# Weight loads, sums and splits lifted above elementwise work in a recurrent layer, and one three-quarter sum loaded earlier

## The chip, the cores and the metric

The kernel runs on one core of a Trainium2 chip. The metric is the device time of one execution in microseconds (us); less is better. The core has five engines with a queue each: TensorE (PE, matrix products), VectorE (DVE) and ScalarE (ACT) for elementwise work, GpSimd (POOL), and SyncE (SP), which here only starts DMA transfers. GpSimd starts transfers too, in this kernel those that add to what lies in the destination.

## The reference

One inference step of a two-layer trunk, for a prompt of 512 frames and 8 decoding sequences of 16 frames, cut here to the recurrent layer that the change touches; the second layer is a stick-breaking attention over a shared key and value cache.

```python
D_MODEL, D_RNN, N_GATE_BLOCKS, CONV_W = 2048, 4096, 16, 4

def recurrent_mixer(hn, h0, conv0, w_in, conv_w, conv_b, w_r, b_r, w_i, b_i, lam, w_out):
    xb, zg = jnp.split(hn @ w_in, 2, axis=-1)          # 2048 -> 2 x 4096
    xb, conv_new = causal_conv(xb, conv0, conv_w, conv_b)
    y, hT = rg_lru(xb, h0, w_r, b_r, w_i, b_i, lam)
    return (y * jax.nn.silu(zg)) @ w_out, hT, conv_new

def rg_lru(x, h0, ...):
    r = jax.nn.sigmoid(block_diag(x, w_r, b_r)); i = jax.nn.sigmoid(block_diag(x, w_i, b_i))
    log_a = -8.0 * r * jax.nn.softplus(-lam)
    a, u = jnp.exp(log_a), jnp.sqrt(-jnp.expm1(2.0 * log_a)) * (i * x)
    # h_t = a_t * h_(t-1) + u_t along the frames
    ...

# per layer: hn = rms_norm(x, g_pre) * (1 + scale) + shift, with (shift, scale, gate) = silu(c) @ w_ada + b_ada  (adaLN)
#            x = x + gate * rms_norm(mixer(hn), g_post)
```

All data are fp32.

## The kernel before

Every fp32 product is made of three matmuls on a split into a high and a low part: high by high (L101), high by low (L102), low by high (L103). `hilo` makes the split of a weight tile: ScalarE writes `wh` (L87), VectorE writes `wl` (L88). Four pairs of `wh`/`wl` are in rotation (`WB = 4`), so splits run at most four tiles ahead of TensorE. `ahead()` draws them from a plan; `weights()` hands out the next one.

The kernel is written in a framework that orders the instructions of each engine at compile time: an instruction goes out by its priority, which follows the order of the code, once its inputs can be there; `high_priority(n)` moves what is written inside it n places up, and `issue_after` holds one instruction behind another. Tiles of one tag share a fixed number of buffers, so a load into a tile waits for the last reader of the tile before.

The stages: a prologue (0 to about 131 us) in which `start` normalises x, reads the adaLN weights (`wa`) and, per block k of 16, projects the first output blocks with `w_first` (`wf`) as they come; the recurrent stage (about 131 to 1080 us); then the output projection and the attention layer, which the change leaves alone.

The recurrent stage works on pairs of feature blocks (256 features), j = 0 to 15: the z-half (`silu_gates`), the recurrence (`lru`) and the x-half (`inputs`) of the next pair with its `conv`. Each half is one `pair_product`: a Winograd scheme for a 2 by 2 block product in seven products instead of eight, on sums of the quarters of the weights. Its order on TensorE is X11, S1, S2, X12, a plain part, S3, X22, a plain part, S4, plain parts. The banks `pa7` and `pc7` are used again, so ScalarE first copies them out (`keep`, L546); VectorE then adds the copies to the other banks (`evac`, to `hb` in the x-half, L616, or to `zs` in the z-half, L661).

The weight sums lie in tiles by tag: `r11` and `r2` one quarter, `t1` and `t3` two, `t2` (x-half) and `u2` (z-half) three, and a fourth later. The first quarter is a plain load on SP's queue (`big_load`, L471), every other one an adding transfer that GpSimd starts (`add`, L476). Two sums into one tile must follow each other. Each tile is loaded again as soon as its split is done. `rv` is the smaller weights.

In `lru`, per block: gates (L689), exponential (L699), tanh (L703) and root (L711) on ScalarE, the scan on VectorE (L723), then

```python
            G.tensor_copy(st[:, h, 0:1], r[:, TP - 1 : TP])                                  # L724
            G.tensor_copy(st[:, h, 1:9], r[:, TP:]...[:, :, TS - 1])                         # L725
            V.tensor_tensor(r, r, zs[h], ALU.mult)                                           # L726
            G.dma_start(self.yd[P * f : P * f + P, :], r)                                    # L727
        G.dma_start(self.O["state"][:, 2 * j : 2 * j + 2, :], st)                            # L728
```

GpSimd copies the final states out of the scan's result (in the trace `st<-g`), and VectorE multiplies that result in place by the gate branch, which has to wait for the copies. The products go to a scratch `yd` in memory. In the trace, tiles appear with their name's first part: `t` is `t1`, `t2` or `t3`, `u` is `u2`, `r` is `r11` or `r2`.

In the prologue, `wf` tiles take the buffers of the first five weight tags (`r11`, `t1`, `t2`, `r2`, `t3`) in turn.

## Time and profile before

| | us |
|---|---|
| three runs | 2930.27, 2933.09, 2934.37 |
| median | 2933.09 |
| the profiled execution | 2927.55 |
| its span | 2925.8 |

The span is what the profile covers from first to last instruction. In the rows of the profile, an engine's row gives busy time, share and count; a stretch gives its length and then the busy time of each engine, the granted TensorE clock (1.00 is full) and the DMA share; a single instruction gives start and duration, and in brackets the idle time before it and what ended that.

### The profile page before, as it was taken

The page shows a single profiled execution, that of the slowest core. Times are in us where ns is not written, and L with a number is a line of the kernel's source. Part 1 is how long each engine was busy: PE and PEld are TensorE (multiplying, and loading weights), DVE is VectorE, ACT ScalarE, POOL GpSimd, SP SyncE. Part 2 cuts the span into 40 slices and gives each one's busy share as a digit, 9 for nine tenths or more (in the row PEclk, how much of TensorE's full clock was granted, in tenths as well). Part 3 has the DMA queues.
Part 4 walks back from the last instruction along what each step waited for, and adds up shares of the span by engine and source line. Part 5 has one row for each costly group of instructions (what it writes and reads, how often), then busy time and mean ns, then how long its engine had stood idle before and what let it go on. Part 6 is the DMA issues. An engine that isn't in the chain of part 4 may idle for free.

```text
span 2925.8 us, 48667 instructions
## 1 busy us (share of the span) xinstructions
PE 2844.2 (97%) x18874; PEld 2532.5 (87%) x18874; DVE 1951.6 (67%) x2795; ACT 1601.4 (55%) x2459; POOL 445.9 (15%) x683
## 2 busy tenths in 40 slices
PE   7889999999999999999999999999999999999998
PEld 5789999999999987778778999878989999897887
DVE  7666776677667766724468877787666766667435
ACT  5456655665556556623456666674455555556323
POOL 0022232222222200001112322001100000001000
PEclk9989999999999999999999999999999999999999
DMA  9967788777777756555567666653665556656736
GB/s 333 328 161 179 178 193 198 173 174 196 192 188 172 180 162 209 175 138 172 175 223 259 215 213 214 206 198 108 198 186 176 182 170 188 193 170 188 218 105 226
DMA packets 263287, 564.07 MB, mean 193 GB/s; under 512 B 24440, under 2 KB 108536, under 8 KB 261904
## 3 DMA queue, kind: packets, MB, share of 16 engines
q1 hardware_dynamic: 232016, 465.60, 50.0%
q0 software_dynamic: 31040, 95.36, 15.6%
q8 instruction: 148, 2.42, 0.3%
q14 instruction: 83, 0.68, 0.1%
HBM read 523.76 MB, written 37.11 MB: 192 GB/s over the span
## 4 chain that ended last, share of the span: by engine, by line
PE 80%; DMA 9%; issue 4%; DVE 4%; POOL 2%; ACT 1%; SPq 0%; DVEq 0%; POOLq 0%; ACTq 0%
PE acc L101 7%; PE acc L102 7%; PE acc L103 7%; PE psh L101 5%; PE acck L101 5%; PE psh L103 5%; PE psh L102 5%; PE acck L103 5%; PE acck L102 5%; DMA u<-w_in_a_dram 4%; PE pa L101 2%; PE pa L103 2%; PE pa L102 2%; DMA t<-w_in_a_dram 2%; PE psa L198 2%
## 5 line engine op out<-in xcount | busy, mean ns | idle before, releaser
L88 DVE TENSOR_TENSOR wl<-wr,wh 128x1024 fp32r<-128x1024 f32 x216 | 269.7, 1249 | 290.6 <-ACT wh L87 287.7
L87 ACT ACTIVATE wh<-wr 128x1024 fp32r<-128x1024 f32 x216 | 228.2, 1056 | 382.4 <-PE acc L103 227.3
L101 PE MATMUL acc<-wh,yh 128*128 128x512 f32 x960 | 378.6, 395 | 8.0 <-ACT yh L764 4.7
L102 PE MATMUL acc<-wl,yh 128*128 128x512 f32 x960 | 377.2, 393 | 6.0 <-DVE wl L88 6.0
L103 PE MATMUL acc<-wh,yl 128*128 128x512 f32 x960 | 375.0, 392 | 1.2 <-DVE yl L765 1.2
L186 DVE TENSOR_TENSOR wa<-wa,wa 128x1024 bf16<-128x1024 f32 (+1 forms) x256 | 310.0, 1246 | 23.6 <-ACT wa L185 21.3
L101 PE MATMUL psh<-nh,wh 128*128 128x320 f32 x1024 | 323.9, 316 | 0.0
L103 PE MATMUL psh<-nh,wl 128*128 128x320 f32 x1024 | 318.9, 311 | 0.0
L102 PE MATMUL psh<-nl,wh 128*128 128x320 f32 x1024 | 317.5, 310 | 0.0
L185 ACT ACTIVATE wa<-wa 128x1024 bf16<-128x1024 f32 x256 | 263.5, 1052 | 60.7 <-DVE wa L186 46.7
L101 PEld LDWEIGHTS acc<-wh,yh 128*128 128x128 f32 x960 | 182.0, 190 | 55.9 <-issue 8.7
L102 PEld LDWEIGHTS acc<-wl,yh 128*128 128x128 f32 x960 | 182.0, 190 | 45.9 <-DVE wl L88 8.7
L103 PEld LDWEIGHTS acc<-wh,yl 128*128 128x128 f32 x960 | 181.4, 189 | 39.9 <-DVE yl L765 2.5
L101 PEld LDWEIGHTS psh<-nh,wh 128*128 128x128 f32 x1024 | 192.3, 188 | 19.3 <-DVE ql L1099 12.6
L101 PE MATMUL pa<-xs,wh 128*128 128x320 f32 x540 | 172.9, 320 | 20.8 <-ACT keep L546 17.5
L103 PEld LDWEIGHTS psh<-nh,wl 128*128 128x128 f32 x1024 | 192.4, 188 | 0.5 <-DVE wl L88 0.2
L102 PEld LDWEIGHTS psh<-nl,wh 128*128 128x128 f32 x1024 | 192.3, 188 | 0.1
L103 PE MATMUL pa<-xs,wl 128*128 128x320 f32 x540 | 169.4, 314 | 5.6 <-DVE wl L88 5.6
L102 PE MATMUL pa<-xs,wh 128*128 128x320 f32 x540 | 169.0, 313 | 0.0
L101 PE MATMUL acck<-nh,wh 128*128 128x320 f32 x512 | 161.5, 315 | 0.0
L476 POOL DMA_DIRECT2D t<-w_in_a_dram x105 | 93.1, 907 | 428.9 <-DMA t<-w_in_a_dram 247.1
L103 PE MATMUL acck<-nh,wl 128*128 128x320 f32 x512 | 158.3, 309 | 0.0
(353 smaller groups left out, 7420.3 us busy)
## 6 DMA issues: line engine op xcount, KB each, us to landing
wa<-w_ada_dram SPq DMA_DIRECT2D x192, 512.0 KB, 4.6
wr<-w_out_a_dram SPq DMA_DIRECT2D x96, 512.0 KB, 4.3
t<-w_in_a_dram POOLq DMA_DIRECT2D x105, 384.0 KB, 7.4
r<-w_in_a_dram SPq DMA_DIRECT2D x90, 384.0 KB, 5.9
wr<-w_in_b_dram SPq DMA_DIRECT2D x64, 512.0 KB, 5.2
ck<-cache_k_dram SPq DMA_DIRECT2D x64, 512.0 KB, 6.5
cv<-cache_v_dram SPq DMA_DIRECT2D x64, 512.0 KB, 5.3
t<-w_in_a_dram SPq DMA_DIRECT2D x75, 384.0 KB, 4.2
```

Of the source, the lines that this page charges most:

```text
L87: nc.scalar.activation(hi[:, :n], raw, AF.Copy)
L88: nc.vector.tensor_tensor(lo[:, :n], raw, hi[:, :n].bitcast(F32), ALU.subtract)
L101: mm(out, sh, mh, start=start, stop=False, **kw)
L102: mm(out, sh, ml, start=False, stop=False, **kw)
L103: mm(out, sl, mh, start=False, stop=stop, **kw)
L185: nc.scalar.activation(parts[i], raw, AF.Copy)
L186: nc.vector.tensor_tensor(parts[2] if i else raw, raw, parts[i], ALU.subtract)
L198: nc.tensor.matmul(ps[32 * j : 32 * j + 32, :], self.c3[:, 4 * g + j, :], ws[j // 2][i][:, j % 2, :], start=g + i == 0, stop=g == 3 and i ...
L476: self.nc.gpsimd.dma_start(t, self.quarter(w, i), accum_op=ALU.add)
```

## The change

Two edits. First, in the prologue, the `wf` tiles no longer use the buffer of `t2`, so that `t2` of the first pair can be loaded, and its two further quarters added, when block 8 of the adaLN weights is reached. The dictionary `big` of loaded tiles is made in `start` for that, and `plan` leaves out a tag that is loaded already. Second, in the recurrent stage, everything that `ahead()` draws from the plan, that is the splits, the loads into the tiles that they free, and the adding transfers, is put into `high_priority(200)`; after that stage the number is 0.

```diff
-        tags = list(self.BIG)[:5]
+        tags = [t for t in self.BIG if t not in ("t2", "u2")]
+        self.big = {}
...
+            if k == 8:
+                self.big_load("t2", self.I["w_in_a"][1])
...
-        self.big = {}
         at = [w[q] for q in order] + [None, None]
         for tag in self.BIG:
-            self.big_load(tag, at[tag == "u2"])
+            if tag not in self.big:
+                self.big_load(tag, at[tag == "u2"])
...
     def ahead(self, held=0):
 
-        for x in islice(self.planned, max(0, self.WB - held - len(self.ready))):
-            self.ready.append(x)
+        with self.tc.high_priority(self.urgent):
+            for x in islice(self.planned, max(0, self.WB - held - len(self.ready))):
+                self.ready.append(x)
...
-            self.WB, self.WW = 4, WQ
+            self.WB, self.WW, self.urgent = 4, WQ, 200
...
-            self.WB, self.RB, self.WW = 3, 4, 1024
+            self.WB, self.RB, self.WW, self.urgent = 3, 4, 1024, 0
```

The changed file's lines stand 2 to 5 further down: L471 becomes L475, L476 L480, L546 L551, L616 L621, L711 L716, L717 L722, L724 to L727 become L729 to L732. The instructions of all engines are the same in both kernels; their order differs. Three places in the recurrence of a middle pair, with the x-half of the next pair on TensorE. The first is GpSimd's queue, where `g_6237` and `g_6272` are the scan results of the pair's two blocks, `t3_6415` and `t2_6442` the weight sums to come. Before:

```order
L476 DMA t1_6227<-w_in_a_dram 128x768 [waits DMASW5_49,DMAHW5_49,DMASW1_49,DVE_49]
L476 DMA t2_5782<-w_in_a_dram 128x768 [waits DMASW3_49,DMASW2_49,DVE_49]
L724 COPY st_5954<-g_6237 128x1 [waits DVE_49]
L725 COPY st_5954<-g_6237 128x8
L727 DMA yd_65<-g_6237 128x640 [waits DVE_49]
L476 DMA t3_6415<-w_in_a_dram 128x768 [waits DMAHW0_49,DMASW6_49,Activation_49]
L724 COPY st_5954<-g_6272 128x1 [waits DVE_49]
L725 COPY st_5954<-g_6272 128x8
L476 DMA t2_6442<-w_in_a_dram 128x768 [waits DMAHW2_49,DMASW2_49,Activation_49]
```

After, at the same place of GpSimd's queue:

```order
L480 DMA t1_6227<-w_in_a_dram 128x768 [waits DMASW4_49,DMAHW5_49,DMASW1_49,DVE_49]
L480 DMA t2_5782<-w_in_a_dram 128x768 [waits DMASW2_49,DVE_49]
L480 DMA t3_6415<-w_in_a_dram 128x768 [waits DMASW6_49,DMAHW0_49,DMASW3_49,DVE_49]
L480 DMA t2_6442<-w_in_a_dram 128x768 [waits DMAHW1_49,DMASW2_49,DVE_49]
L729 COPY st_5954<-g_6237 128x1 [waits DVE_49]
L730 COPY st_5954<-g_6237 128x8
L732 DMA yd_65<-g_6237 128x640 [waits DVE_49]
L480 DMA t2_6442<-w_in_a_dram 128x768 [waits DMASW4_49]
L729 COPY st_5954<-g_6272 128x1 [waits DVE_49]
L730 COPY st_5954<-g_6272 128x8
```

The sums of the coming `t3` and `t2` moved up past the state copies, and the second sum of `t2`, which waits for the first to land (DMASW4), now stands ahead of the copies of the second block. The second place is VectorE's queue from the second block's scan on. Before:

```order
L723 SCALAR_TENSOR_TENSOR g_6272<-q_6320,g_6272 128x640 [waits DVE_49]
L616 TENSOR_TENSOR hb_6359<-pb7_6448,keep_6391 128x320 [waits PE_49]
L88 TENSOR_TENSOR wl_6506<-rv_6133,wh_6505 128x512 [waits DMAHW2_49,PE_49,Activation_49]
L726 TENSOR_TENSOR g_6272<-g_6272,zs_5982 128x640 [waits DVE_49,Pool_49]
L88 TENSOR_TENSOR wl_6512<-r11_6196,wh_6511 128x768 [waits DMAHW4_49,PE_49,Activation_49]
```

After, on VectorE's queue:

```order
L728 SCALAR_TENSOR_TENSOR g_6272<-q_6320,g_6272 128x640 [waits DVE_49]
L88 TENSOR_TENSOR wl_6506<-rv_6133,wh_6505 128x512 [waits DMAHW2_49,PE_49,Activation_49]
L731 TENSOR_TENSOR g_6272<-g_6272,zs_5982 128x640 [waits DVE_49,Pool_49]
L88 TENSOR_TENSOR wl_6512<-r11_6196,wh_6511 128x768 [waits DMAHW4_49,PE_49,Activation_49]
L621 TENSOR_TENSOR hb_6359<-pd7_6486,keep_6517 128x192 [waits PE_49]
L88 TENSOR_TENSOR wl_6538<-t1_6227,wh_6537 128x768 [waits DMASW1_49,Activation_49]
```

The in-place product of the second block (L726, now L731) keeps its place after the scan and its wait for GpSimd; the splits behind it moved up towards it. The third place is ScalarE's queue in the roots of the same pair, where `keep_6391` and `keep_6418` are the first two copies of the x-half, and `t3_6033` and `t2_5782` the weights of its S1 and S2. Before:

```order
L711 ACTIVATE g_6237<-g_6237 128x640 [waits DVE_49]
L711 ACTIVATE g_6272<-g_6272 128x640 [waits DVE_49,Activation_49]
L546 ACTIVATE keep_6391<-pa7_6365 128x320 [waits PE_49]
L87 ACTIVATE wh_6411<-t3_6033 128x768 [waits DMASW6_49,PE_49]
L717 ACTIVATE q_6318<-q_6318,mone_101 128x640 [waits DVE_49]
L717 ACTIVATE q_6320<-q_6320,mone_101 128x640 [waits DVE_49]
L546 ACTIVATE keep_6418<-pc7_6366 128x320 [waits PE_49]
L87 ACTIVATE wh_6438<-t2_5782 128x768 [waits DMASW2_49,PE_49]
```

After, on ScalarE's queue:

```order
L87 ACTIVATE wh_6411<-t3_6033 128x768 [waits DMASW6_49,PE_49]
L716 ACT_TABLE_LOAD
L716 ACTIVATE g_6237<-g_6237 128x640 [waits DVE_49]
L87 ACTIVATE wh_6438<-t2_5782 128x768 [waits DMASW2_49,PE_49]
L716 ACTIVATE g_6272<-g_6272 128x640 [waits DVE_49,Activation_49]
L551 ACTIVATE keep_6391<-pa7_6365 128x320
L722 ACTIVATE q_6318<-q_6318,mone_101 128x640 [waits DVE_49]
L551 ACTIVATE keep_6418<-pc7_6366 128x320
```

Both splits moved up, that of `t3` ahead of the roots and that of `t2` between them and ahead of the first `keep`.

## The prediction

> **What bounds the kernel now.** I read the page's head and its first table, then the stretches of the span by engine, then the waits and single rows of the recurrent stage, since the diff touches only the prologue and that stage. The page first.

> ```profile
> span 2925.8 us, 48667 instructions
> PE 2844.2 (97%) x18874; PEld 2532.5 (87%) x18874; DVE 1951.6 (67%) x2795; ACT 1601.4 (55%) x2459; POOL 445.9 (15%) x683
> ```

> TensorE is busy for 97% of the span, so a change in order can gain only what TensorE waits, and lose by new waits. Where it waits, by stretch (start:end, length, then busy time of each engine, granted clock, DMA share, GB/s):

> ```profile
> 131.00:160.00 29.00, 19.14 (x103) 18.48 (x102) 15.45 (x45) 11.60 (x23) 8.92 (x18) 0.82 0.94 214
> 185.00:240.00 55.00, 48.68 (x308) 47.44 (x307) 43.46 (x67) 39.31 (x58) 9.74 (x17) 0.91 0.56 137
> 540.00:600.00 60.00, 59.13 (x401) 58.63 (x401) 42.69 (x67) 35.26 (x54) 16.22 (x27) 1.00 0.76 185
> 600.00:660.00 60.00, 57.99 (x394) 57.50 (x393) 41.53 (x63) 35.20 (x53) 13.29 (x22) 1.00 0.74 178
> ```

> Two places lose: the first product (131 to 160), and the first whole pair (185 to 240). The steady stage loses 1 to 2 us in each 60. The waits of TensorE between 131 and 1075 us (total, times, longest):

> ```profile
> PE pa L101 <- ACT keep L546: 17.5, 14, 6.5
> PE pa L103 <- DVE wl L88: 5.6, 1, 5.6
> PE pa L101 <- ACT hb L611: 3.4, 1, 3.4
> ```

> The 14 waits on the copy `keep` are one of 6.50 us in the prologue and 13 of one kind, one in each later pair: 17.5 - 6.5 = 11.0 us, or 0.85 each. What a wait costs beside its own length shows in rows of single gaps (the bracket holds the idle time) and in the stretches of halved clock behind them:

> ```profile
> 140.63 0.41 PE L101 MATMUL pa<-xs,wh 128*128 128x320 f32 x1 [3.36 <-ACT hb L611]
> 154.20 0.64 PE L101 MATMUL pa<-xs,wh 128*128 128x320 f32 x1 [6.50 <-ACT keep L546]
> 204.31 0.63 PE L103 MATMUL pa<-xs,wl 128*128 128x320 f32 x1 [5.57 <-DVE wl L88]
> 621.24 0.42 PE L101 MATMUL pa<-xs,wh 128*128 128x320 f32 x1 [2.01 <-ACT keep L546]
> 1066.75 0.71 PE L101 MATMUL acc<-wh,yh 128*128 128x512 f32 x1 [2.49 <-ACT yh L764]
> ```

> ```profile
> 141.85:145.27 3.42, 3.42 (x15) 3.42 (x14) 0.93 (x6) 0.16 (x1) 0.82 (x5) 0.50 1.05 276
> 152.09:158.92 6.83, 4.72 (x18) 4.72 (x19) 5.73 (x8) 3.94 (x9) 2.66 (x6) 0.50 0.93 193
> 199.88:210.12 10.24, 5.81 (x22) 5.81 (x23) 10.00 (x17) 2.98 (x5) 4.15 (x10) 0.50 0.52 148
> 1066.87:1070.28 3.41, 3.41 (x9) 2.63 (x10) 3.41 (x9) 3.41 (x5) 0.00 (x0) 0.50 0.21 77
> 619.30:640.00 20.70, 18.76 (x128) 18.76 (x129) 10.17 (x14) 11.08 (x18) 2.59 (x3) 1.00 0.80 205
> ```

> After gaps of 2.49 us and more the granted clock is 0.50 for 3.4 us or a multiple of it; after the gap of 2.01 us it stays 1.00. At full clock matmuls of this shape start 0.147 us apart (18.76 us / 128), so 3.42 us hold 23; the first row has 15. A gap of some 2.5 to 4.5 us therefore costs about 8 x 0.147 = 1.2 us more.

> **The change, part by part.** The instructions are the same in number and kind; only the order changes, and only up to the end of the recurrent stage at some 1075 us. So every term is a wait won or lost.

> *Steady pairs, 13 of them (j = 1 to 13).* I take the pair whose x-half (`inputs`) starts on TensorE at E = 580.99, and count from there. GpSimd's queue carries both the adding transfers of the weights and the copies of the recurrence's state:

> ```profile
> 582.13 1.76 POOL L476 DMA_DIRECT2D t<-w_in_a_dram  x2 [7.41 <-DMA t<-w_in_a_dram]
> 595.24 0.91 POOL L724 COPY st<-g 128x1 f32<-128x1 f32 x1 [11.35 <-DVE h0t L720]
> 599.56 0.19 POOL L724 COPY st<-g 128x1 f32<-128x1 f32 x1 [0.62 <-DVE g L723]
> 602.39 0.87 POOL L476 DMA_DIRECT2D t<-w_in_a_dram  x1 [2.52 <-ACT wh L87]
> 610.18 0.90 POOL L476 DMA_DIRECT2D t<-w_in_a_dram  x1 [5.42 <-DMA t<-w_in_a_dram]
> 610.76 1.25 POOL L476 DMA_DIRECT2D u<-w_in_a_dram  x1
> ```

> ```profile
> 580.99 0.31 PE L101 MATMUL pa<-xs,wh 128*128 128x320 f32 x1
> 600.39 0.82 DVE L726 TENSOR_TENSOR g<-g,zs 128x640 f32<-128x640 f32 x1
> 610.48 0.42 ACT L546 ACTIVATE keep<-pa 128x320 f32<-128x320 f32 x1
> 612.03 0.31 PE L101 MATMUL pa<-xs,wh 128*128 128x320 f32 x1
> ```

> Before, both pairs of state copies (595.24 and 599.56) are through before the first sum of the next `t2` goes out (602.39). Its second sum goes out at 610.18, when the first has landed; since the same tile is summed twice, this wait is real. Behind it stand only the `u2` sum and others: that is the cause of the 2.01 us gap at 621.24, as the chain of waits shows, where the `u2` sum lands at 619.92 and its split and the `keep` follow:

> ```profile
> 602.39 7.23 DMA t<-w_in_a_dram
> 610.76 9.16 DMA u<-w_in_a_dram
> 620.77 0.43 ACT keep L546
> ```

> After, as the order of GpSimd shows, both sums of `t2` are pulled ahead of the second block's state copies. The second sum waits for the landing of the first with the copies behind it, and VectorE's second `g *= zs` (L726, then L731) waits for these copies: it overwrites what they read. Behind it on VectorE, in order, stand the splits, convolution steps and `hb` evictions that the z-half (`silu_gates`) needs. When does it run? Five steps, with these rows for the durations:

> ```profile
> t<-w_in_a_dram POOLq DMA_DIRECT2D x105, 384.0 KB, 7.4
> t<-w_in_a_dram SPq DMA_DIRECT2D x75, 384.0 KB, 4.2
> DMA to landing us min/median/max: 3.2/6.8/10.6
> L87 ACT ACTIVATE wh<-t x90: 827/842/849, 139.4 to 1030.1; 128x768 fp32r<-128x768 f32 x90
> L88 DVE TENSOR_TENSOR wl<-t,wh x90: 940/951/961, 140.2 to 1031.4; 128x768 fp32r<-128x768 f32 x90
> ```

> 1. The present `t2` must be split before its tile is free. Its last sum is the second of the two at 582.13, issued about 0.57 later (as 610.76 stands behind 610.18): 582.7 + 7.4 = 590.1. Split on ScalarE 0.84 and VectorE 0.95: 591.9, E + 11.0. It cannot be earlier.
> 2. The load of the next `t2` takes 4.2 and GpSimd's start some 0.6: first sum issued at E + 15.8.
> 3. From its issue to that of the second sum 610.18 - 602.39 = 7.8: E + 23.6.
> 4. The copies follow one issue later (0.58, from 610.18 to 610.76), and L726 started 600.39 - 599.56 = 0.83 after the copies began: E + 25.0. Before it was 600.39, E + 19.4.
> 5. From L726 to the end of `keep` in the z-half it was 610.90 - 600.39 = 10.5. In the new order one more split (0.95) stands between: 11.45. So `keep` ends at E + 36.45.

> TensorE wants that `keep` at 612.03, E + 31.04. The x-half, too, loses something: on ScalarE the split of `t2` now stands between the two square roots and ahead of the first `keep`, so this `keep` ends no sooner than E + 9.1 (landing) + 0.84 + 0.69 (root, half of the 1.37 below) + 0.42 = 11.05, while TensorE gets there after 66 to 68 matmuls, E + 9.7 to 10.0.

> ```profile
> 588.44 1.37 ACT L711 ACTIVATE g<-g 128x640 f32<-128x640 f32 x2
> ```

> That is 1.0 us (0 if the sum lands 1.4 earlier, 2.5 if 1.5 later). TensorE then arrives at E + 32.0 and waits 36.45 - 32.0 = 4.4 us. Per pair: 4.4 + 1.2 for the halved clock + 1.0, less the present gap of 0.85, whose cause goes: +5.75 us, and 13 x 5.75 = **+75 us**. The bounds of step 2 and 3: with 3.2 for the load and a sum that lands in 5.8, `keep` ends 2.6 us earlier and the wait is 1.8, under the gap that halved nothing: (1.8 + 1.0 - 0.85) x 13 = +25. With 5.6 for the load and 10.6 for the sum the wait is 9 and the sum +135; I take the medians, since two of these sums in the rows above took 7.2 and 7.8 with all waits.

> [...]

> *The first pair (j = 0).* The gap of 5.57 us at 204.31 is VectorE's: a split stood behind scans. With the lift it goes ahead of them. But the same inversion on GpSimd holds the state copies there too, with one product fewer on TensorE behind which the delay could hide; I cost it at 0, with the bounds -7 (gap 5.57 and, of 4.67 us at halved clock, 22 matmuls instead of 32, 1.4) and +4.

> *The prologue.* Three `rv` loads, `r11`, `t1`, `r2`, the `t2` base and its two sums move ahead of the last adaLN weights. The DMA share is 0.95 there:

> ```profile
> 23.00:131.00 108.00, 100.95 (x933) 75.73 (x934) 73.47 (x209) 50.37 (x94) 1.20 (x1) 1.00 0.95 339
> ```

> So nothing is hidden: at 339 GB/s a load of 384 KB is 1.2 us of DMA time and one of 256 KB 0.8; three of the latter, `r11`, `t1`, `r2`, the `t2` base and its two sums make some 9 us by which adaLN's last weights come later. In return the splits of `t1` and `t2` no longer wait. On SP's queue the loads of `r11`, `t1` and `r2` wait for tiles that the last `wf` used, with adaLN loads behind them. At most the two gaps and their halved clock go (3.36 + 6.50 + 1.2 + 2.1 = 13.2); at worst 9 us come on top. I take 0.

> Sum: 2927.55 (the profiled execution) + 75 + 0 + 0 = 3003. The median of the runs is 2933.09, 5.5 above that execution and about as much as I can resolve; I leave the sum at 3003, since no term is known that closely.

> **Rivals.**
> *Faster, since the cover holds.* If L731 starts by E + 20.5, `keep` ends as TensorE arrives, and nothing is lost. This needs load and first sum together in some 6.7 us instead of 12; the fastest single transfer of `t`, 3.2, would make it possible, the median 6.8 speaks against it. Then the 11.0 us of steady gaps go, the 7 of the first pair and half of the prologue's 13.2: 2927.55 - 24.6 = 2903. [...]
> *Slower by little.* Transfers at their fast end: +25, without halved clock, 2953.
> *Same.* The wait per pair is about as long as the old gap (L731 at E + 21): 2925 to 2935.
> *The change does not do what it says:* excluded as far as the order goes, which does move.

> **How the numbers follow.** Forecast, a wait of over 2.5 us in each pair: 0.68, 2965 to 3040. Slower by little: 0.14. Same: 0.07. Faster: 0.11. Two tenths of a per cent, about 6 us, is what a measurement here can tell from no change. So faster 0.11, same 0.07, slower 0.82. The range from 2935 to 3035 leaves out the faster case, part of the same, and the slowest end, where transfers take 9 us and more.

> **What would show it.** In the waits after: VectorE `g` L731 waiting on GpSimd's L730 for 4 us or more, 13 times; TensorE `pa` on `keep` L551 up from 0.85 to some 4.4 us in each pair; halved clock once per pair; 60-us windows with TensorE at 54 to 56 us. On GpSimd a `t` sum waiting for a `t` landing just ahead of L729. Step 3 is wrong if that landing takes under 5 us; step 5 is wrong if VectorE catches up in under 8 us. The prologue's term is wrong if the first product's S2 does not start within 150 to 160 us. If L731 runs before E + 20.5, the whole forecast fails.

## The result and the profile after

The changed kernel takes 3003.2 us (median; 3001.74 to 3004.97) against 2931.7 before, a ratio of 1.0244 (95% interval 1.0226 to 1.0262). Its profiled execution took 3003.07 us with a span of 3001.0. So 71.5 us lie between the medians and 75.5 between the two profiled executions. The head of its page, and the stretches that answer to those of before (same columns):

```profile
span 3001.0 us, 48659 instructions
PE 2866.8 (96%) x18874; PEld 2549.3 (85%) x18874; DVE 1955.1 (65%) x2795; ACT 1603.1 (53%) x2459; POOL 427.1 (14%) x683
131.00:160.00 29.00, 22.85 (x160) 19.84 (x156) 15.34 (x52) 12.03 (x24) 3.88 (x9) 0.91 0.77 204
185.00:240.00 55.00, 51.27 (x342) 49.92 (x341) 42.01 (x64) 41.02 (x62) 10.47 (x20) 1.00 0.69 164
540.00:600.00 60.00, 55.36 (x364) 54.60 (x363) 40.46 (x61) 32.23 (x50) 12.73 (x25) 0.97 0.71 168
600.00:660.00 60.00, 55.18 (x363) 54.42 (x363) 40.46 (x62) 34.28 (x51) 11.78 (x24) 0.97 0.69 165
```

The share of TensorE is only a point lower, but the steady stretches of 60 us now hold 364 matmuls instead of some 400, and the clock is below 1.00 in them. The waits between 131 and 1160 us name the place:

```profile
PE pa L101 <- ACT keep L551: 62.4, 30, 4.9
DVE g L731 <- POOL st L730: 60.4, 23, 5.3
POOL t L480 <- DMA t<-w_in_a_dram: 298.4, 48, 10.6
```

Before, TensorE waited 17.5 us for `keep`; VectorE's waits for GpSimd's state copies (before: L726 for L725) came to 4.0 us there and are 60.4 now. In a pair whose x-half starts at E = 550.64, GpSimd, VectorE, ScalarE and TensorE read:

```profile
550.64 0.31 PE L101 MATMUL pa<-xs,wh 128*128 128x320 f32 x1
561.30 0.42 PE L101 MATMUL pa<-xs,wh 128*128 128x320 f32 x1 [0.39 <-ACT keep L551]
565.80 0.86 POOL L480 DMA_DIRECT2D t<-w_in_a_dram  x1 [2.48 <-DVE h0t L725]
566.34 0.52 POOL L729 COPY st<-g 128x1 f32<-128x1 f32 x1
573.57 0.86 POOL L480 DMA_DIRECT2D t<-w_in_a_dram  x1 [4.84 <-DMA t<-w_in_a_dram]
574.11 0.51 POOL L729 COPY st<-g 128x1 f32<-128x1 f32 x1
574.78 0.83 DVE L731 TENSOR_TENSOR g<-g,zs 128x640 f32<-128x640 f32 x1 [4.95 <-POOL st L730]
586.27 0.41 ACT L551 ACTIVATE keep<-pa 128x320 f32<-128x320 f32 x1
586.74 0.45 PE L101 MATMUL pa<-xs,wh 128*128 128x320 f32 x1 [4.25 <-ACT keep L551]
586.90:590.50 3.60, 3.60 (x15) 3.60 (x16) 3.11 (x5) 0.84 (x2) 0.25 (x2) 0.53 1.00 207
```

The first sum of `t2` goes out at 565.80; the second waits for its landing and goes out at 573.57; the second block's copy comes behind it; VectorE, idle for 4.95 us, multiplies at 574.78; `keep` ends at 586.68, TensorE has waited 4.25 us, and the next 3.6 us run at a clock of 0.53 (the last row is a stretch of the span).

Four pieces make up the 75.2 us between the two spans. They are taken by the starts of S1 (the first matmul into `pc`) in the x-halves, since after the change four matmuls of one X11 run some 5 us ahead of the others. Up to the first pair's recurrence it is +8.8 (186.51 to 195.33), in the first pair -5.0 (so that the next S1 starts at 232.82 instead of 229.01), in the 13 steady pairs +68.1 (840.7 instead of 772.5 from that start to the last one's), and +3.3 after them. There the order is the same, and the ten profiles of this case differ by as much: from the start of the last x-half to the end they take 1926 to 1931 us.

### The profile page after: what moved, and what is told of

Its sections match the earlier page's. It is cut to its first block, busy times and chain, and to the rows that moved or that the text cites. A ratio compares the mean times of both kernels' runs of the same rounds, so it can differ in the third digit from the quotient of the medians.

```text
span 3001.0 us, 48659 instructions
## 1 busy us (share of the span) xinstructions
PE 2866.8 (96%) x18874; PEld 2549.3 (85%) x18874; DVE 1955.1 (65%) x2795; ACT 1603.1 (53%) x2459; POOL 427.1 (14%) x683
## 4 chain that ended last, share of the span: by engine, by line
PE 76%; DMA 8%; DVE 7%; ACT 4%; issue 3%; POOL 1%; SPq 0%; DVEq 0%; POOLq 0%; ACTq 0%
PE acc L101 6%; PE acc L102 6%; PE acc L103 6%; PE psh L101 5%; PE acck L101 5%; PE psh L103 5%; PE psh L102 5%; PE acck L102 5%; PE acck L103 5%; DMA t<-w_in_a_dram 3%; DVE wl L88 3%; PE pa L101 2%; DMA wa<-w_ada_dram 2%; PE pa L102 2%; PE pa L103 2%
## 5 line engine op out<-in xcount | busy, mean ns | idle before, releaser
L88 DVE TENSOR_TENSOR wl<-wr,wh 128x1024 fp32r<-128x1024 f32 x216 | 269.4, 1248 | 287.6 <-ACT wh L87 284.6
L87 ACT ACTIVATE wh<-wr 128x1024 fp32r<-128x1024 f32 x216 | 228.2, 1056 | 381.3 <-PE acc L103 222.5
L101 PE MATMUL acc<-wh,yh 128*128 128x512 f32 x960 | 379.3, 396 | 8.8 <-ACT yh L769 5.3
L103 PE MATMUL acc<-wh,yl 128*128 128x512 f32 x960 | 375.5, 393 | 1.0 <-DVE yl L770 1.0
L186 DVE TENSOR_TENSOR wa<-wa,wa 128x1024 bf16<-128x1024 f32 (+1 forms) x256 | 310.1, 1246 | 23.4 <-ACT wa L185 21.1
L101 PE MATMUL psh<-nh,wh 128*128 128x320 f32 x1024 | 323.9, 316 | 0.0
L103 PE MATMUL psh<-nh,wl 128*128 128x320 f32 x1024 | 318.9, 311 | 0.0
L185 ACT ACTIVATE wa<-wa 128x1024 bf16<-128x1024 f32 x256 | 263.3, 1052 | 60.4 <-DVE wa L186 46.0
L101 PE MATMUL pa<-xs,wh 128*128 128x320 f32 x540 | 179.9, 333 | 62.0 <-ACT keep L551 60.9
L101 PEld LDWEIGHTS acc<-wh,yh 128*128 128x128 f32 x960 | 182.1, 190 | 56.7 <-issue 8.7
L103 PEld LDWEIGHTS acc<-wh,yl 128*128 128x128 f32 x960 | 182.0, 190 | 40.3 <-DVE yl L770 2.4
L101 PEld LDWEIGHTS psh<-nh,wh 128*128 128x128 f32 x1024 | 192.3, 188 | 19.3 <-DVE ql L1104 12.6
L103 PEld LDWEIGHTS psh<-nh,wl 128*128 128x128 f32 x1024 | 192.4, 188 | 0.5 <-DVE wl L88 0.2
L480 POOL DMA_DIRECT2D t<-w_in_a_dram x105 | 91.2, 868 | 623.3 <-DMA t<-w_in_a_dram 398.8
L102 PE MATMUL pa<-xs,wh 128*128 128x320 f32 x540 | 174.8, 324 | 0.0
L103 PE MATMUL pa<-xs,wl 128*128 128x320 f32 x540 | 174.7, 324 | 0.0
L101 PEld LDWEIGHTS pa<-xs,wh 128*128 128x128 f32 x540 | 108.4, 201 | 71.5 <-ACT keep L551 68.8
L101 PE MATMUL acck<-nh,wh 128*128 128x320 f32 x512 | 161.5, 315 | 0.0
## 6 DMA issues: line engine op xcount, KB each, us to landing
t<-w_in_a_dram POOLq DMA_DIRECT2D x105, 384.0 KB, 6.2
r<-w_in_a_dram SPq DMA_DIRECT2D x90, 384.0 KB, 5.4
t<-w_in_a_dram SPq DMA_DIRECT2D x75, 384.0 KB, 3.6
```

Of the source, the lines that this page charges most:

```text
L87: nc.scalar.activation(hi[:, :n], raw, AF.Copy)
L88: nc.vector.tensor_tensor(lo[:, :n], raw, hi[:, :n].bitcast(F32), ALU.subtract)
L101: mm(out, sh, mh, start=start, stop=False, **kw)
L102: mm(out, sh, ml, start=False, stop=False, **kw)
L103: mm(out, sl, mh, start=False, stop=stop, **kw)
L185: nc.scalar.activation(parts[i], raw, AF.Copy)
```

## The experiments

All eight kernels differ from the changed kernel only in the lines shown or named. The first four take the change apart, the last four look for a better version.

**Everything lifted but the sums.**

```diff
     def add(self, t, w, i):
-        self.nc.gpsimd.dma_start(t, self.quarter(w, i), accum_op=ALU.add)
+        with self.tc.high_priority(-self.urgent):
+            self.nc.gpsimd.dma_start(t, self.quarter(w, i), accum_op=ALU.add)
```

> The changed kernel, except that the adding transfers keep their old priority; splits and plain loads stay lifted, the early t2 too. On GpSimd this alone puts the second sum of t2 back behind the second block's state copies. Theory (the second sum holds the copies, these hold VectorE's second product): that product starts near E + 19.5 instead of 24, the wait of TensorE at S2 of the z-half (3.5 to 4.7 us in each pair) goes and with it the halved clock; some 13 x 5.5 = 70 us come back: 2925 to 2940. Rival (the splits lifted on ScalarE and VectorE delay the convolution and the keeps): the wait stays at 2 us or more in each pair, 2970 to 3003.

Measured: 2933.1 us, ratio 1.0005 (0.9996 to 1.0015) to before. On GpSimd in the steady pairs the second sum of `t2` now stands behind the second copy; its rows (here E = 532.74), VectorE's product, TensorE's waits for `keep` and a steady stretch:

```profile
547.91 0.87 POOL L481 DMA_DIRECT2D t<-w_in_a_dram  x1 [2.37 <-DVE h0t L726]
551.41 0.19 POOL L730 COPY st<-g 128x1 f32<-128x1 f32 x1 [0.58 <-DVE g L729]
551.76 0.82 DVE L732 TENSOR_TENSOR g<-g,zs 128x640 f32<-128x640 f32 x1 [0.41 <-POOL st L731]
555.45 0.86 POOL L481 DMA_DIRECT2D t<-w_in_a_dram  x1 [3.72 <-DMA t<-w_in_a_dram]
PE pa L101 <- ACT keep L552: 13.4, 17, 4.6
540.00:600.00 60.00, 59.61 (x405) 59.12 (x404) 43.45 (x66) 36.76 (x55) 14.97 (x25) 1.00 0.76 185
```

The product runs at E + 19.0 instead of 24.1, and each of 12 pairs takes 59.0 us, a little less than before (58.8 to 60.6) and 4 to 8 less than after (62.8 to 66.8). The splits' new order on ScalarE and VectorE costs only the 0.39 us in the x-half, which stays. The rival fell. That the total is still no better than before lies ahead of these pairs: the prologue is late as in the changed kernel, and in the first steady pair, whose sums of `t2` still stand ahead of the copies, the product runs at E + 22.5 and the pair takes 63.1 us.

**A smaller first sum, same order.**

```diff
-                self.add(t, w, i)
+                c = P if tag == "t2" and n == 1 else WQ
+                self.nc.gpsimd.dma_start(t[:, :c], self.quarter(w, i)[:, :c], accum_op=ALU.add)
```

> The changed kernel, but the first sum of t2 adds only 128 of the 768 columns, so part of that weight sum is left out; the order on every engine is the same as in the changed kernel. Theory (the price is the landing of that sum, during which the copies stand behind the second one): it lands in some 3 to 4 us instead of 7, VectorE's second product starts near E + 20, the wait in each pair falls under 0.5 us, 2925 to 2945. Rival (the order on GpSimd, VectorE or ScalarE costs as such, whatever the landing): no more than 15 us come back, 2985 to 3003.

Measured: 2933.8 us, ratio 1.0005 (0.9993 to 1.0017). With the order of the changed kernel kept, but one of its transfers at 64 instead of 384 KB (first row: median 4.2 us to landing), the loss is gone. This kernel leaves out five sixths of that sum, so it serves for its time alone. The pair at E = 528.76:

```profile
t<-w_in_a_dram POOLq DMA_DIRECT2D x14, 64.0 KB, 4.2
544.09 0.87 POOL L478 DMA_DIRECT2D t<-w_in_a_dram  x1 [2.68 <-DVE h0t L726]
548.55 0.86 POOL L478 DMA_DIRECT2D t<-w_in_a_dram  x1 [1.53 <-DMA t<-w_in_a_dram]
549.76 0.83 DVE L732 TENSOR_TENSOR g<-g,zs 128x640 f32<-128x640 f32 x1 [1.15 <-POOL st L731]
```

From issue to issue it takes 4.46 us instead of 7.77, and the product runs at E + 21.0, just early enough: over the 12 pairs from the second on it runs at E + 20.6 to 22.7, and TensorE waits there only where it is later than 21.4 (0.28 us at 21.6, 1.39 at 22.7). So the copies' place in the queue costs no wait of itself; the landing time that they stand behind does, from about E + 21.4 on.

**Only the early `t2`** (`self.urgent` 0 throughout).

> Only the first edit: t2 of the first pair is loaded and summed during the adaLN weights, nothing is lifted. Theory: the steady pairs are as before (E to E 58.8 to 60.6 us, one gap of 0.2 to 2.0 us); only the prologue moves, its second wait (6.5 us on the split of t2's sums) shrinks and adaLN's weights come 3 to 5 us later: 2922 to 2938. Rival (the early load is what delays the prologue in the changed kernel by 9 us): E of the first pair at 190 to 194, 2938 to 2943.

Measured: 2934.7 us, ratio 1.001 (0.9998 to 1.0021). The prologue's second wait shrinks and the first grows:

```profile
147.43 0.64 PE L101 MATMUL pa<-xs,wh 128*128 128x320 f32 x1 [4.96 <-ACT hb L616]
157.34 0.42 PE L101 MATMUL pa<-xs,wh 128*128 128x320 f32 x1 [1.72 <-ACT keep L551]
```

The first was 3.36 us at 140.63, the second 6.50 at 154.20. The first pair's recurrence starts at 184.7 on TensorE against 183.9. So what the early load gives and takes is the same to 0.8 us; it isn't what delayed the changed kernel's prologue.

**Only the lift** (`tags` and the place of `t2` as before).

> Only the second edit: all that is drawn from the plan is lifted, t2 comes at its old place. Theory: the steady pairs lose as in the changed kernel, 5.2 us each (65 us per pair), and the prologue is late since SP's loads of r11, t1, t2 and r2 stand ahead of the last adaLN weights and wait there for the splits of the tiles before: 2995 to 3015. Rival (the early t2 has a part in the steady loss or makes the prologue's): under 2990.

Measured: 3011.1 us, ratio 1.027 (1.0248 to 1.0293): the whole loss. Whether it is more than in the changed kernel is not shown, since its four runs lie between 3002.7 and 3020.2 and the intervals overlap. In the profiled run, the slowest of the four, the pairs take 64.4 to 67.2 us (61.8 the first). Waits of TensorE from 131 us on:

```profile
PE pa L101 <- ACT keep L549: 67.8, 28, 5.0
PE pss L223 <- DMA wa<-w_ada_dram: 10.6, 2, 6.6
```

The second row is adaLN's: its weights come late, as they do in the changed kernel. Why shows on SP, in the changed kernel (with TensorE's longest wait for these weights) and before it:

```profile
123.03 0.33 SPq L475 DMA_DIRECT2D t<-w_in_a_dram  x1
123.45 0.86 SPq L221 DMA_DIRECT2D wa<-w_ada_dram  x2
129.96 0.65 PE L223 MATMUL pss<-wa,cT 128*32 128x256 f32 x4 [6.09 <-DMA wa<-w_ada_dram]
125.04 1.72 SPq L221 DMA_DIRECT2D wa<-w_ada_dram  x3
136.21 0.33 SPq L475 DMA_DIRECT2D r<-w_in_a_dram  x1
136.64 0.37 SPq L221 DMA_DIRECT2D wa<-w_ada_dram  x1
```

```profile
120.26 1.95 SPq L221 DMA_DIRECT2D wa<-w_ada_dram  x3
122.26 0.42 SPq L387 DMA_DIRECT2D wf<-w_first_dram  x1
```

Before, the last adaLN load goes out by 122.2, and TensorE's longest wait for one between 60 and 131 us is 1.47. After, two weight loads of the pairs stand ahead of adaLN loads, each waiting for its tile: `t1` from 116.0 to 123.0, for which TensorE pays with 6.09 us at 129.96, and `r2` from 126.8 to 136.2, so that the last adaLN load goes out at 136.64.

**Sums not lifted, and the lift only behind the first product.**

```diff
-            self.WB, self.WW, self.urgent = 4, WQ, 200
+            self.WB, self.WW, self.urgent = 4, WQ, 0
...
         block = self.conv(0, ep, *self.inputs(0, ep))
+        self.urgent = 200
```

> As the run without lifted sums, and the splits and loads are lifted only once the first product's code is behind, so that the prologue's loads keep their places; t2 is still loaded early. Theory (the prologue lost 9 to 13 us since r11, t1 and r2 stood on SP's queue ahead of the last adaLN weights, waiting there for splits): the first pair's x-half starts at 218 to 224 us instead of 233.7, the steady pairs stay at 59.0 us: 2918 to 2926. Rival (the early t2 itself, by its DMA time, made the prologue late): 2928 to 2935.

Measured: 2923.1 us, ratio 0.9968 (0.9954 to 0.9983): by 0.3% faster than the kernel before, and the fastest here together with the next one. The kernel also has the edit of the first experiment. On SP the last adaLN loads are out by 126.4, not only at 136.6:

```profile
119.40 6.95 SPq L221 DMA_DIRECT2D wa<-w_ada_dram  x4
126.40 0.42 SPq L391 DMA_DIRECT2D wf<-w_first_dram  x1
```

The first whole pair's x-half starts at 224.1 (233.7 with the lifted prologue, 226.4 before).

**The same without the early `t2`.**

> As the run before it, without the early t2. Theory (the early t2 moves bytes in a stretch that the DMA bounds, and gains and loses about as much): within 3 us of the run with it, 2918 to 2927. Rival (the early t2 takes away the prologue's waits): 5 us or more slower than with it.

Measured: 2924.8 us, ratio 0.9964 (0.995 to 0.9979). With and without the early load is the same within the intervals, as the early load alone had shown.

**A lift of 60 places, and one of 30** (`self.urgent = 60` or `30` in the sixth kernel, in place of 200).

> As the run without the early t2, with a lift of 60 places instead of 200. The first two pairs' sums of t2 and u2 then stand behind the state copies too, which the lift of 200 still puts ahead of them there, and in the x-half the split for S2 stands behind both roots, ahead of the first keep. Theory: the waits of 2.4 and 1.0 us of the first pair go with their halved clock, 3 to 5 us, and the 0.39 us in each x-half stays or grows to at most 1: 2914 to 2924. Rival (the lift must be large for the u2 sums to come in time): a wait of 0.5 us or more returns at S3 of the z-half, 2925 to 2935.

> The same with a lift of 30 places: on ScalarE the split for S2 in the x-half stands behind the first keep, so the 0.39 us there can go, as before the change. Theory: the steady pairs come to 58.6 to 59.0 us, 2910 to 2922. Rival: the splits are late again on VectorE in the first pair (the gap of 5.6 us returns), 2922 to 2935.

Measured: 2927.1 us, ratio 0.9974 (0.9964 to 0.9985), and 2932.4 us, ratio 0.9997 (0.9986 to 1.0007). Both expectations of the theory were too low, and both times lie in the rivals' ranges, though the wait that the first rival named is not among the waits and the gap that the second named came back only in part. TensorE's waits, two rows of the first and two of the second:

```profile
PE pd L101 <- ACT wh L87: 10.4, 15, 2.8
PE pa L101 <- ACT keep L550: 7.6, 2, 7.3
PE pa L101 <- ACT keep L550: 10.4, 7, 5.2
PE pc L101 <- ACT wh L87: 6.9, 14, 0.5
```

The place of the 0.39 us in the x-half moves (to a split that TensorE awaits at `pd`, or at `pc`), but it grows to 0.5 in every pair; and the first pair's gap on VectorE, which the larger lift removed, returns in part (with 30 places 1.61 and 0.85 us on VectorE's splits, beside 2.36 on a `keep`). What was hoped from the sums of the first two pairs was smaller than that.

## Why the prediction was right, step by step

The total, 3003 against 3003.2, is nearer than its terms.

- *Steps 1 to 4, the second product on VectorE.* Forecast E + 25.0; in the pair shown E + 24.1, over the 12 pairs 23.4 to 24.8. The sum's issue was forecast at E + 15.8, it is 15.16; the time to the next issue 7.8, it is 7.77. One wait in step 2 is another than forecast: the load lands at 565.25, and the row's bracket names VectorE's `h0t`, which ends at 565.71; so by the trace VectorE held the sum for the last 0.5 us. That this mechanism carries the loss is shown from both sides: the order changed with the transfers as they are, and one transfer changed with the order as it is.
- *Step 5.* 11.45 us forecast from that product to the end of `keep`, 11.90 measured (574.78 to 586.68).
- *TensorE's wait.* Forecast 4.4, measured 3.5 to 4.7 with a mean of 3.9 in 12 pairs and 2.5 in the first.
- *The x-half.* Forecast 1.0, measured 0.39. The last sum of the present `t2` goes out at 551.07, E + 0.4, and not at E + 1.7 as taken from the row of before, since the splits ahead of it are lifted too; it lands at E + 7.7 instead of 9.1, and its split then waits only for its turn on ScalarE.
- *The halved clock.* Forecast 1.2 per pair. Idle time in the 13 pairs is 56.8 us after and 11.0 before, so 45.8 of the 68.1 us are idle. Nearly all of the other 22.3, or 1.7 per pair, is clock: the matmuls in the halved stretches come 20.5 us later than at the distance of 0.147 us. Two of the 12 long gaps halve nothing, four halve 6.8 us, the others 3.4.
- *The sum per pair.* Forecast +5.75, measured 5.2 (59.4 to 64.7 on average). The waits were put a little too high, the clock too low.
- *The prologue.* Forecast 0 with -13 to +9, and it came out at +8.8. The term was mis-sized: it named the loads that wait on SP ahead of adaLN, but priced them by their bytes, some 9 us, and netted that against the saved waits. What came was the wait itself, 7.0 and 9.4 us on SP's queue, so that the +8.8 lies near the bound of 9 by luck. The saved waits did not go: the first is 1.20 instead of 3.36 us, but a new one of 2.84 stands ahead of it, the wait for S2 there is still 4.86 us, and S2 starts at 163.8, outside the 150 to 160 that the prediction set as its mark.
- *The first pair.* Forecast 0, measured -5.0: the gap of 5.57 us on a late split is gone, as the rival for a gain had it. The two errors cancel to +3.8, which with the +3.3 of the rest makes up what the pairs lost less (68.1 instead of 75). So the mechanism was right, and that the total fits to 1 us was luck.
- *The rivals.* The faster case, in which the cover holds, asked for the product by E + 20.5; the run with the small sum shows the limit near 21.4, and what the kernel does then: 2933.8, no gain, as the rival "same" had it for a product at E + 21. Of the terms behind 2903 only the first pair's came, with 5 of 7 us. The old gaps do go in that run and in the one without lifted sums, but the 0.39 us in each x-half and waits of 2.7 and 3.4 us in the first steady pair take their place, so that 9.1 and 8.1 of the 11.0 us stay; and the prologue lost 8.5 us in the first of these runs, where it was to gain 6.6.

## What to carry to other kernels

A priority that is given to a whole chain (splits, loads, sums) also moves its members in queues that the chain shares with others. Before lifting an instruction, look at what it waits for at its new place and who stands behind it: here an issue that takes 0.9 us held two small copies for 5 us, since its tile was still being summed, and two loads held another stage's weights for 7 and 9 us. Lift only the members whose inputs are there, and start the lift behind the stage that the queue is still serving.

## What the runs showed of the hardware

In the two profiles of the kernels before and after, the clock does not halve at a fixed length of gap. Between 131 and 1160 us, 3 of 8 gaps of TensorE of 2.0 to 3.52 us halved it, and all 13 from 3.55 us on. The same gap of 2.49 us at the start of the output projection halves it in both; in the kernel with the later lift it does not, and neither does a gap of 3.52 us in the changed kernel, as the stretches behind the two show:

```profile
1062.30 0.50 PE L101 MATMUL acc<-wh,yh 128*128 128x512 f32 x1 [2.49 <-ACT yh L771]
1062.30:1066.30 4.00, 3.21 (x13) 2.32 (x14) 4.00 (x9) 3.59 (x5) 0.00 (x0) 1.00 0.21 73
394.21 0.41 PE L101 MATMUL pa<-xs,wh 128*128 128x320 f32 x1 [3.52 <-ACT keep L551]
394.20:398.20 4.00, 3.99 (x27) 3.99 (x28) 3.29 (x5) 1.02 (x2) 0.25 (x2) 1.00 0.98 206
```

```profile
389.01:392.42 3.41, 1.68 (x12) 1.42 (x10) 2.67 (x6) 0.67 (x2) 2.12 (x6) 1.00 0.20 23
392.42:395.84 3.42, 1.63 (x11) 1.63 (x12) 3.29 (x5) 2.80 (x6) 0.19 (x3) 1.00 0.97 179
1063.45:1066.87 3.42, 0.93 (x5) 0.46 (x4) 3.33 (x4) 3.41 (x5) 0.00 (x0) 1.00 0.11 22
1066.87:1070.28 3.41, 3.41 (x9) 2.63 (x10) 3.41 (x9) 3.41 (x5) 0.00 (x0) 0.50 0.21 77
```

The grid lies elsewhere in the two executions (its first step begins 1.9 us after the start of the span before, 3.3 us after it in the changed kernel). So in this case a gap of between 1.9 and some 3.7 us (twice 1.85, between 1.81 and 1.89; an estimate from these counts) halves the clock in some places and not in others.

By the medians between 131 and 1160 us, in the run with the small sum, a sum of 64 KB by an adding transfer takes 4.2 us to land and those of 384 KB into `t` 6.1: a sixth of the bytes, but 4.2 of the 6.1 us.
